# Second norm to up projection: S1 formed from PSUM, S4 in one pass, low parts shared out differently, and the tensor engine's order written out

## The chip, the cores and the metric

The kernel runs on one core of one Trainium2 chip. Five engines of that core work side by side, each through a queue of its own: the tensor engine (PE; its weight loads are listed as PEld), the vector engine (DVE), the scalar engine (ACT), GpSimd (POOL), and SP, which issues the DMAs. The metric is the device time of one execution in microseconds. Before the change it is 2224.81 us, the median of three runs (2224.61 to 2228.78).

## The reference

The program is two layers of an encoder over 1024 tokens of 1024 channels. The part that matters here is the second half of each layer:

```python
x = x + mix @ w_out[l]
h2 = _rmsnorm(x, norm2_g[l])
up = _dwconv3(h2 @ ffn_w_up[l], ffn_conv_w[l])
gate, val = jnp.split(up, 2, axis=-1)
x = x + (jax.nn.silu(gate) * val) @ ffn_w_down[l]
```

`ffn_w_up` has 1024 rows and 2 × 2816 columns. `_dwconv3` is a convolution of three taps along the tokens, one set of taps for each column.

## The kernel before

**Seven products in place of eight.** The product h2 @ W_up is done tile by tile. Tile f (of 22) holds 128 gate columns and the 128 value columns that belong to them. The transposed activations are cut into four quadrants: A11 and A12 are the lower and the upper 512 channels of tokens 0 to 511, A21 and A22 the same channels of tokens 512 to 1023. The weights of a tile are cut likewise: B11 and B21 are the lower and upper channels of the gate columns, B12 and B22 those of the value columns. The scheme is Winograd's form of Strassen's: with S1 = A21 + A22, S2 = S1 − A11, S3 = A11 − A21, S4 = A12 − S2 and T1 = B12 − B11, T2 = B22 − T1, T3 = B22 − B12, T4 = B21 − T2, a tile takes the seven products A11·B11, A12·B21, S1·T1, S2·T2, S3·T3, S4·B22 and A22·T4.

**Three passes for each product.** Each operand is split (`split`, line 114) into a high part, a copy rounded to a narrower type that ACT makes (line 106), and a low part, the rest, a subtraction that DVE or POOL makes (line 117). The kernel multiplies high by high, high by low and low by high (`block_mm`, line 869, its matmuls on line 876): four blocks of 128 channels times three passes, twelve matmuls of 128×512 for each product. They add up in PSUM: S1·T1 and S4·B22 in one bank (`c5`), A11·B11, S2·T2, S3·T3 and A22·T4 in another (`u`), with copies taken in between (`p1`, `u1`, `p5`).

**From the norm to the quadrants.** `norm2_step` (line 822) runs over eight blocks of 128 tokens. For each it does the second half of the output projection (`out_proj`), and, one block behind, the norm (`norm_a`: squares on ACT, line 256, the root on POOL, the multiply on DVE, line 262), and, two blocks behind, `norm2_b` (line 777), which transposes a block through PSUM (line 781) and makes the quadrants. Blocks 0 to 3 give A11 and A12. Blocks 4 to 7 give A22, which is split at once from PSUM, S3 and S2 (DVE, lines 797 and 798), and S1 and S4 (POOL, lines 799 and 800). These sums lie unsplit in two buffers of 8 × 512: `r0` holds A11 and A12, which S1 and S4 overwrite, and `r1` holds S3 and S2. `norm2_end` (line 802) then splits each of S2, S1, S3, S4 in two pieces of 128×1024. Later `r1` serves tile 0 as working storage (`ug`, `uv`, `tg`, `tv`), so that its copies overwrite S2 and S3.

**The weights.** `up_load` (line 836) brings a tile's weights in on SP in two DMAs of 512 KB. `up_prep` (line 852) forms T1 to T4 in place on POOL (line 864; T2 overwrites T1, T4 overwrites B21) and splits them (`up_split`). The low part is made on DVE or on POOL, as the argument `el` says.

**What sets the order.** A planner orders each engine's queue from its own estimates. Within `manual_schedule` the named engines keep the order in which the program is written. `run` (lines 1194 to 1212) does this for DVE, POOL and ACT from block 7's norm to tile 1's weights; the tensor engine's order there is the planner's. In that section tile 0's and tile 1's first two products, which need blocks 0 to 3 alone, are written ahead (`up_ahead`, `up_ahead_copy`), and tile 0 is run as a generator in three parts. What follows, the rest of tile 0 with its convolution (`conv3`, lines 452 to 457) and all other tiles, is ordered by the planner again.

Of the kernel before, what the change touches and what calls it, by code (L numbers as in the profile page):

```python
# [10 lines left out]
AF = mybir.ActivationFunctionType  # L11
ALU = mybir.AluOpType
# [44 lines left out]
class Trunk:  # L57
# [719 lines left out]
    def norm2_b(self, b, xs):  # L777
        nc = self.nc
        pt = self.big()
        for k in range(KC):  # L780
            nc.tensor.transpose(
                pt[:, k * P : (k + 1) * P], xs[:, k * P : (k + 1) * P], self.ident
            )
        pv = pt.rearrange("p (k t) -> p k t", k=KC)
        s = slice((b % 4) * P, (b % 4 + 1) * P)
        r0, r1 = self.raw
        if b == 4:
            self.A["22"] = self.slot(self.xo[0], [2, 4, 512], F32R)
        if b < 4:
            nc.scalar.activation(r0[:, :, s], pv, AF.Copy)  # L790
        for n, k in (("11", 0), ("12", 4)) if b < 4 else (("22", 4),):
            h, l = self.A[n][:, 0, :, s], self.A[n][:, 1, :, s]
            self.split(h, l, pv[:, k : k + 4, :], "a", "v")
        if b >= 4:

            a11, a12, s3, s2 = r0[:, 0:4, s], r0[:, 4:8, s], r1[:, 0:4, s], r1[:, 4:8, s]
            nc.vector.tensor_tensor(out=s3, in0=a11, in1=pv[:, 0:4, :], op=ALU.subtract)
            nc.vector.tensor_tensor(out=s2, in0=pv[:, 4:8, :], in1=s3, op=ALU.subtract)
            nc.gpsimd.tensor_tensor(out=a11, in0=s2, in1=a11, op=ALU.add)
            nc.gpsimd.tensor_tensor(out=a12, in0=a12, in1=s2, op=ALU.subtract)  # L800

    def norm2_end(self, names):

# [18 lines left out]
    def norm2_step(self, b, xs, g, xout):  # L822
        self.out_proj(b, 1)
        self.nc.sync.dma_start(xout[b], self.x[b])
        if b >= 1:
            xs[b - 1] = self.norm_a(b - 1, self.x[b - 1], g, ("G1", "G5"))
        if b >= 2:
            self.norm2_b(b - 2, xs[b - 2])

    def a_op(self, n, k):  # L830
        t = self.A[n]
# [20 lines left out]
    def up_prep(self, f, raws, steps=("11", "T1", "T2", "21", "T3", "22", "T4")):  # L852


        b11, b21, b12, b22 = raws
        B = self.B.setdefault(f, {})
        of = {"11": b11, "T1": b11, "T2": b11, "21": b21, "T3": b12, "22": b22, "T4": b21}
        subs = {"T1": (b12, b11), "T2": (b22, b11), "T3": (b22, b12), "T4": (b21, b11)}
        for n in steps:
            t = n.upper()  # L860
            if t in subs and t not in self.formed.setdefault(f, set()):
                p, q = subs[t]
                self.formed[f].add(t)
                self.nc.gpsimd.tensor_tensor(out=of[t], in0=p, in1=q, op=ALU.subtract)  # L864
            if n == t:
                early = f < 2 and n in ("11", "21")
                B[n] = self.up_split(of[n], "v" if early or n in ("11", "T2", "T3") else "p")

    def block_mm(self, out, a, B, first, last):

# [9 lines left out]

    def up_ahead(self, f, B):

        u, c2 = self.acc("pa"), self.acc(("po", "pf")[f])
        self.block_mm(u, "11", B["11"], True, False)
        self.block_mm(c2, "12", B["21"], True, True)
        return u, c2

    def up_ahead_copy(self, f, u, c2):
        if f == 0:
            self.p1 = self.S(GK)  # L890
        p1 = self.p1[:, f * 512 : f * 512 + 512]
        self.nc.scalar.activation(p1, u, AF.Copy)
        return u, c2, p1

    def up_tile(self, f, B, ahead=None, L=None):

# [2 lines left out]
        nc = self.nc  # L899
# [11 lines left out]
        if ahead:  # L911
            u, c2, p1 = ahead
# [21 lines left out]
        if L is not None:  # L934

            self.order = ExitStack()
            self.order.enter_context(self.tc.manual_schedule(engines={mybir.EngineType.SP}))
            self.down_begin(L)
        self.block_mm(c5, "S4", B["22"], False, True)
        add(uv[:, lo], c5, u1)  # L940
        self.block_mm(u, "22", B["T4"], False, True)
        cp(ug[:, hi], u)

        cg, cv = self.big(), self.big()
        self.conv3(cv, uv, scales(NFF + f))
# [180 lines left out]
    def run(self, depth):  # L1126
# [6 lines left out]
        for L in range(depth):  # L1133
# [57 lines left out]
                elif b == 4:  # L1191
                    self.up_prep(0, raws[0], ("11", "21", "T1", "t2", "t3", "t4"))
            raws[1] += self.up_load(L, 1, (1,))
            with self.tc.manual_schedule(engines=MANUAL):
                xs[7] = self.norm_a(7, self.x[7], g2, ("G1", "G5"))
                ahead.append(self.up_ahead(0, self.B[0]))
                self.up_prep(1, raws[1], ("11", "21"))
                self.norm2_b(6, xs[6])
                ahead[0] = self.up_ahead_copy(0, *ahead[0])
                self.up_prep(0, raws[0], ("T2",))  # L1200
                self.norm2_b(7, xs[7])
                self.up_prep(0, raws[0], ("T3",))
                ahead.append(self.up_ahead(1, self.B[1]))
                ahead[1] = self.up_ahead_copy(1, *ahead[1])
                self.norm2_end(("S2", "S1", "S3"))
                first = self.up_tile(0, self.B[0], ahead[0])
                next(first)
                self.up_prep(0, raws[0], ("22", "T4"))
                self.norm2_end(("S4",))
                self.up_prep(1, raws[1], ("t1",))  # L1210
                next(first)
# [86 lines left out]
```

## Time and profile before

| | |
|---|---|
| median of three runs | 2224.81 us (2224.61 to 2228.78) |
| profiled execution, its own time | 2225.25 us |
| profiled execution, span | 2223.4 us |
| granted tensor clock, mean | 0.999 |
| PE busy | 2202.3 us (99%) |
| DVE busy | 1511.4 us (68%) |
| POOL busy | 1156.9 us (52%) |
| ACT busy | 1106.9 us (50%) |

Times in the profile count from the start of the span. The edited section of layer 0 lies at about 470 to 515 us, that of layer 1 at about 1573 to 1618 us. A row of the timeline gives the start, the length, the engine, the line, the operation, what it writes and reads by the names of the buffers, how many instructions are merged in the row, and in brackets how long its engine was idle before it and what ended that. The names are those of the slots: in this section E and G are weights or pieces of them, H are the large activation buffers, `big`, `pa`, `po` and `pf` are PSUM, and the pieces of S2 lie in W and Z, those of S1 in H, those of S3 and S4 in G and W.

### The profile page before, as it was taken

Reading aid. Unit: us, or ns where it says so; the run is one execution under the profiler, and the core shown is the slowest. Engines: PE = TensorE matmul, PEld = TensorE weight load, DVE = VectorE, ACT = ScalarE, POOL = GpSimd, SP = SyncE. Lnnn points to the kernel's source line nnn. Section 1 sums busy time; section 2 is a strip of 40 time slices with the busy share of each in tenths; the row PEclk is TensorE's granted clock in tenths of the full one; section 3 lists DMA queues with packets and bytes.
Section 4 is the critical chain, followed back from the end, with each engine's and each line's share of the span. In section 5 each row is a group of like instructions: output and inputs, shape, how many; then the busy total and the mean of one; then the engine's idle time right before and its main releaser. Section 6 shows DMA issues by size and latency. Waiting matters only on the chain.

```text
span 2223.4 us, 29441 instructions
## 1 busy us (share of the span) xinstructions
PE 2202.3 (99%) x10590; PEld 1829.1 (82%) x10590; DVE 1511.4 (68%) x1945; ACT 1106.9 (50%) x1879; POOL 1156.9 (52%) x1060
## 2 busy tenths in 40 slices
PE   9999999999999999999999999999999999999999
PEld 7888888877888888888888888888788888888887
DVE  5668887177677777754735688862877777778554
ACT  5247776365444444433432477753545454544332
POOL 5564445577767776020443653556777777751100
PEclk9999999999999999999999999999999999999999
DMA  4100003213545453886520000041235545548754
GB/s 159 45 20 5 16 15 97 109 67 109 167 160 162 156 170 121 296 313 214 203 90 10 20 15 6 21 149 58 76 119 157 171 148 166 161 142 322 281 193 164
DMA packets 202020, 281.91 MB, mean 127 GB/s; under 512 B 15598, under 2 KB 121618, under 8 KB 201874
## 3 DMA queue, kind: packets, MB, share of 16 engines
q1 hardware_dynamic: 201874, 280.03, 37.5%
q8 instruction: 83, 1.36, 0.3%
q14 instruction: 63, 0.52, 0.1%
HBM read 199.77 MB, written 80.22 MB: 126 GB/s over the span
## 4 chain that ended last, share of the span: by engine, by line
PE 85%; POOL 4%; DVE 3%; DMA 3%; issue 2%; ACT 1%; SPq 0%; POOLq 0%; DVEq 0%; ACTq 0%
PE pa L876 17%; PE pf L876 8%; PE big L1075 8%; PE pa L1075 5%; PE pa L638 5%; PE pf L301 5%; PE po L876 4%; PE big L622 3%; PE big L621 3%; PE po L650 3%; PE po L651 3%; PE po L1075 2%; PE pf L1075 2%; PE pa L132 2%; PE pa L130 2%; PE pa L131 2%
## 5 line engine op out<-in xcount | busy, mean ns | idle before, releaser
L630 POOL TENSOR_SCALAR H<-H,rv 128x1024 f32<-128x1024 f32 x128 | 144.6, 1130 | 221.8 <-DVE rv L629 221.8
L876 PE MATMUL pa<-H,E 128*128 128x512 f32 x864 | 212.7, 390 | 1.1 <-DVE H L909 1.1
L643 DVE TENSOR_TENSOR E<-pa,E 128x512 fp32r<-128x512 f32 x256 | 173.4, 688 | 52.2 <-ACT E L642 50.8
L106 ACT ACTIVATE E<-E 128x512 fp32r<-128x512 f32 (+1 forms) x207 | 128.6, 628 | 157.0 <-POOL E L864 72.5
L117 POOL TENSOR_TENSOR E<-E,E 128x512 fp32r<-128x512 f32 (+1 forms) x120 | 176.5, 1475 | 53.0 <-ACT E L106 52.6
L642 ACT ACTIVATE E<-pa 128x512 fp32r<-128x512 f32 x256 | 152.8, 597 | 79.8 <-PE pa L638 78.3
L876 PEld LDWEIGHTS pa<-H,E 128*128 128x128 f32 x864 | 161.6, 188 | 35.3 <-DVE H L909 2.0
L106 ACT ACTIVATE G<-H 128x1024 fp32r<-128x1024 f32 (+1 forms) x116 | 114.1, 1008 | 143.7 <-PE big L1075 73.0
L117 DVE TENSOR_TENSOR G<-H,G 128x1024 fp32r<-128x1024 f32 (+1 forms) x86 | 105.0, 1224 | 110.3 <-ACT G L106 109.9
L624 DVE TENSOR_REDUCE nm<-big 128x1 f32<-128x1024 f32 x128 | 155.7, 1216 | 8.1 <-PE big L622 8.0
L910 ACT ACTIVATE H<-pa 128x512 f32<-128x512 f32 x128 | 75.9, 593 | 167.9 <-PE pa L876 126.7
L638 PEld LDWEIGHTS pa<-ident,H 128*128 128x128 f32 x1024 | 127.1, 140 | 35.4 <-DVE E L643 1.6
L638 PE MATMUL pa<-ident,H 128*128 128x128 f32 x1024 | 154.0, 272 | 0.2
L627 ACT ACTIVATE H<-big,nm 128x1024 f32<-128x1024 f32 x128 | 142.4, 1112 | 12.3 <-DVE nm L624 12.2
L453 DVE SCALAR_TENSOR_TENSOR big<-H,cst,big 128x1023 f32<-128x1023 f32 x44 | 56.6, 1287 | 105.7 <-ACT big L452 105.7
L117 DVE TENSOR_TENSOR E<-E,E 128x512 fp32r<-128x512 f32 (+1 forms) x92 | 96.3, 1055 | 38.2 <-ACT E L106 38.2
L301 PE MATMUL pf<-H,G 128*128 128x512 f32 x288 | 120.1, 431 | 0.0
L876 PE MATMUL pa<-W,E 128*128 128x512 f32 x336 | 116.1, 394 | 0.8 <-ACT H L910 0.5
L994 POOL TENSOR_TENSOR E<-E 128x512 f32<-128x512 f32 x26 | 37.0, 1425 | 140.2 <-DMA E<-in_ffn_w_down_dram 139.9
L106 ACT ACTIVATE G<-E 128x512 fp32r<-128x512 f32 (+2 forms) x110 | 58.5, 546 | 98.2 <-POOL E L864 29.9
L876 PE MATMUL po<-H,E 128*128 128x512 f32 x408 | 104.4, 390 | 0.4 <-ACT E L106 0.4
L864 POOL TENSOR_TENSOR E<-E 128x512 f32<-128x512 f32 x66 | 100.5, 1524 | 3.1
(408 smaller groups left out, 6367.1 us busy)
## 6 DMA issues: line engine op xcount, KB each, us to landing
H<-gdram SPq DMA_DIRECT2D x70, 512.0 KB, 5.6
gdram<-H SPq DMA_DIRECT2D x134, 256.0 KB, 2.5
E<-in_ffn_w_up_dram SPq DMA_DIRECT2D x66, 512.0 KB, 4.4
H<-tdram SPq DMA_DIRECT2D x40, 512.0 KB, 5.2
E<-in_w_in_dram SPq DMA_DIRECT2D x30, 512.0 KB, 3.9
H<-in_ffn_w_down_dram SPq DMA_DIRECT2D x30, 512.0 KB, 4.6
out_dram<-H SPq DMA_DIRECT2D x28, 512.0 KB, 2.9
E<-in_ffn_w_down_dram SPq DMA_DIRECT2D x26, 512.0 KB, 6.4
```

Source lines behind the costliest of these rows:

```text
L106: nc.scalar.activation(out, in_, AF.Copy)
L117: e.tensor_tensor(out=l, in0=src, in1=h.bitcast(F32), op=ALU.subtract)
L301: mm(acc, a[:, k, :], b, start=k + j == 0, stop=k == KC - 1 and j == 2)
L624: nc.vector.tensor_reduce(out=nm, in_=S, op=ALU.max, axis=AX.X, negate=True)
L627: nc.scalar.activation(p, S, AF.Exp, bias=nm, accum_out=sm)
L630: nc.gpsimd.tensor_scalar(out=p, in0=p, scalar1=rv, scalar2=1.0, op0=ALU.mult, op1=ALU.mult)
L638: nc.tensor.transpose(pt[:, r * P : (r + 1) * P], pu[:, r, kc * P : (kc + 1) * P], self.ident)
L642: nc.scalar.activation(hl[:, 0, :], pt, AF.Copy)
L643: nc.vector.tensor_tensor(out=hl[:, 1, :], in0=pt, in1=hl[:, 0, :].bitcast(F32), op=ALU.subtract)
L864: self.nc.gpsimd.tensor_tensor(out=of[t], in0=p, in1=q, op=ALU.subtract)
L876: mm(out, w, x, start=first and k + j == 0, stop=k == 3 and j == 2, skip_group_check=True,)
L1075: nc.tensor.matmul(banks[j], p[:, n, s], r[:, n, :], start=first and n + q == 0 and m < 3, stop=last and n == w - 1 and q == 2, skip_group ...
```

## The change

There are five edits, all in the section between the second norm and the second tile of the up projection, once per layer.

- `norm2_b` for blocks 4 to 7 no longer has POOL add S2 to A11 to get S1. ACT copies A21 out of PSUM over A11, and DVE adds A22 from PSUM to it. S3 and S2 come first, the copy and the addition second, and the split of A22 third. The function is a generator now, so that the three steps can be placed apart.
- S4 is no longer formed block by block. `norm2_s4` subtracts S2 from A12 on POOL in four operations of 128×512, one for each block of channels, after all blocks are done. S4 is split last.
- The low parts of the weights are shared out differently. Tile 0: B11 and B21 on DVE, all others on POOL (T2 and T3 were on DVE). Tile 1: T1, T2, T3 and B22 on DVE, B11, B21 and T4 on POOL (B11, B21, T2 and T3 were on DVE).
- `manual_schedule` covers the tensor engine as well, and `up_ahead` is a generator. The written order is: block 6's transposes, tile 0's two products ahead, block 7's transposes, tile 1's two products ahead, S2·T2, S1·T1.
- In tile 0, A22·T4 comes ahead of S4·B22.

```diff
@@ norm2_b
-        for n, k in (("11", 0), ("12", 4)) if b < 4 else (("22", 4),):
+        for n, k in (("11", 0), ("12", 4)) if b < 4 else ():
             h, l = self.A[n][:, 0, :, s], self.A[n][:, 1, :, s]
             self.split(h, l, pv[:, k : k + 4, :], "a", "v")
         if b >= 4:
-            a11, a12, s3, s2 = r0[:, 0:4, s], r0[:, 4:8, s], r1[:, 0:4, s], r1[:, 4:8, s]
+            a11, s3, s2 = r0[:, 0:4, s], r1[:, 0:4, s], r1[:, 4:8, s]
             nc.vector.tensor_tensor(out=s3, in0=a11, in1=pv[:, 0:4, :], op=ALU.subtract)
             nc.vector.tensor_tensor(out=s2, in0=pv[:, 4:8, :], in1=s3, op=ALU.subtract)
-            nc.gpsimd.tensor_tensor(out=a11, in0=s2, in1=a11, op=ALU.add)
-            nc.gpsimd.tensor_tensor(out=a12, in0=a12, in1=s2, op=ALU.subtract)
+            yield
+            nc.scalar.activation(a11, pv[:, 0:4, :], AF.Copy)
+            nc.vector.tensor_tensor(out=a11, in0=pv[:, 4:8, :], in1=a11, op=ALU.add)
+            yield
+            self.split(
+                self.A["22"][:, 0, :, s], self.A["22"][:, 1, :, s], pv[:, 4:8, :], "a", "v"
+            )
+
+    def norm2_s4(self):
+        r0, r1 = self.raw
+        for k in (6, 5, 4, 7):
+            self.nc.gpsimd.tensor_tensor(
+                out=r0[:, k], in0=r0[:, k], in1=r1[:, k], op=ALU.subtract
+            )
@@ up_prep
-                early = f < 2 and n in ("11", "21")
-                B[n] = self.up_split(of[n], "v" if early or n in ("11", "T2", "T3") else "p")
+                dve = (("11", "21"), ("T1", "T2", "T3", "22"))[f] if f < 2 else ("11", "T2", "T3")
+                B[n] = self.up_split(of[n], "v" if n in dve else "p")
@@ up_ahead (up_ahead_copy is gone)
-        u, c2 = self.acc("pa"), self.acc(("po", "pf")[f])
+        u = self.acc("pa")
         self.block_mm(u, "11", B["11"], True, False)
-        self.block_mm(c2, "12", B["21"], True, True)
-        return u, c2
...
+        yield
         self.nc.scalar.activation(p1, u, AF.Copy)
-        return u, c2, p1
+        yield
+        c2 = self.acc(("po", "pf")[f])
+        self.block_mm(c2, "12", B["21"], True, True)
+        yield u, c2, p1
@@ up_tile
+        if f == 0:
+            self.block_mm(u, "22", B["T4"], False, True)
+            cp(ug[:, hi], u)
         self.block_mm(c5, "S4", B["22"], False, True)
         add(uv[:, lo], c5, u1)
-        self.block_mm(u, "22", B["T4"], False, True)
-        cp(ug[:, hi], u)
+        if f > 0:
+            self.block_mm(u, "22", B["T4"], False, True)
+            cp(ug[:, hi], u)
@@ run
-            with self.tc.manual_schedule(engines=MANUAL):
+            with self.tc.manual_schedule(engines=MANUAL | {mybir.EngineType.PE}):
                 xs[7] = self.norm_a(7, self.x[7], g2, ("G1", "G5"))
-                ahead.append(self.up_ahead(0, self.B[0]))
                 self.up_prep(1, raws[1], ("11", "21"))
-                self.norm2_b(6, xs[6])
-                ahead[0] = self.up_ahead_copy(0, *ahead[0])
+                part = [self.norm2_b(b, xs[b]) for b in (6, 7)]
+                next(part[0])
+                next(part[0])
+                begun = [self.up_ahead(f, self.B[f]) for f in range(2)]
+                next(begun[0])
+                next(begun[0])
+                ahead.append(next(begun[0]))
                 self.up_prep(0, raws[0], ("T2",))
-                self.norm2_b(7, xs[7])
+                next(part[1])
+                next(part[0], None)
+                next(part[1])
+                self.norm2_end(("S2",))
                 self.up_prep(0, raws[0], ("T3",))
-                ahead.append(self.up_ahead(1, self.B[1]))
-                ahead[1] = self.up_ahead_copy(1, *ahead[1])
-                self.norm2_end(("S2", "S1", "S3"))
+                next(begun[1])
+                next(begun[1])
+                ahead.append(next(begun[1]))
+                self.norm2_s4()
+                self.up_prep(0, raws[0], ("T4", "22"))
+                self.norm2_end(("S1",))
+                next(part[1], None)
+                self.norm2_end(("S3",))
                 first = self.up_tile(0, self.B[0], ahead[0])
                 next(first)
-                self.up_prep(0, raws[0], ("22", "T4"))
                 self.norm2_end(("S4",))
                 self.up_prep(1, raws[1], ("t1",))
                 next(first)
```

4 lines of the change are left out of this document (2 added, 2 removed).

## The prediction

> **What bounds the kernel now.** I read the page first.
>
> ```profile
> span 2223.4 us, 29441 instructions
> PE 2202.3 (99%) x10590; PEld 1829.1 (82%) x10590; DVE 1511.4 (68%) x1945; ACT 1106.9 (50%) x1879; POOL 1156.9 (52%) x1060
> ```
>
> The tensor engine is busy 99% of the span, so an edit to other engines is worth only what it takes out of the tensor engine's waits. Next I took the busy time by windows around the edited code: the stretch from the first matmul of tile 0's "11" product to the first matmul of tile 1's S2·T2, in layer 0 and in layer 1, and then slices of it.
>
> ```profile
> 478.88:513.00 34.12, 30.71 (x139) 23.61 (x137) 32.60 (x31) 21.14 (x32) 25.05 (x17) 1.00 0.21 62
> 1582.30:1616.05 33.75, 31.51 (x139) 25.02 (x138) 30.84 (x31) 19.78 (x29) 23.72 (x16) 0.95 0.20 63
> ...
> 474.00:478.00 4.00, 4.00 (x19) 3.30 (x18) 3.75 (x4) 0.93 (x2) 2.90 (x4) 1.00 0.32 131
> ...
> 490.00:494.00 4.00, 2.38 (x10) 1.41 (x8) 3.88 (x4) 3.17 (x4) 4.00 (x4) 1.00 0.00 0
> ...
> 502.00:506.00 4.00, 3.34 (x12) 2.10 (x12) 4.00 (x3) 0.57 (x1) 3.40 (x2) 1.00 0.81 228
> ...
> 1598.00:1602.00 4.00, 4.00 (x12) 3.13 (x11) 4.00 (x4) 2.41 (x3) 0.70 (x1) 0.57 0.00 0
> ```
>
> The columns are time, then busy time of PE, PEld, DVE, ACT, POOL, granted clock, DMA. Here DVE is the full engine (32.60 of 34.12 us), and PE has holes (2.38 of 4.00). The timeline of layer 0 (start, length, engine) shows what the holes wait for:
>
> ```profile
> 478.88 2.58 PEld L876 LDWEIGHTS pa<-H,E 128*128 128x128 f32 x12
> ...
> 481.77 1.29 DVE L262 SCALAR_TENSOR_TENSOR G<-H,rsx,E 128x1024 f32<-128x1024 f32 x1
> ...
> 482.98 3.48 DVE L117 TENSOR_TENSOR E<-E,E 128x512 fp32r<-128x512 f32 x2
> ...
> 485.56 0.60 ACT L106 ACTIVATE H<-big 128x512 fp32r<-128x512 f32 x1 [3.69 <-PE big L781]
> ...
> 486.06 1.02 PEld L781 LDWEIGHTS big<-ident,G 128*128 128x128 f32 x8
> ...
> 487.05 2.14 PEld L876 LDWEIGHTS pa<-H,E 128*128 128x128 f32 x10
> ...
> 488.29 0.68 DVE L117 TENSOR_TENSOR E<-E,E 128x512 fp32r<-128x512 f32 x1
> ...
> 490.08 1.30 POOL L800 TENSOR_TENSOR H<-H,H 128x512 f32<-128x512 f32 x1
> ...
> 490.20 0.69 DVE L798 TENSOR_TENSOR H<-big,H 128x512 f32<-128x512 f32 x1
> ...
> 490.93 2.01 ACT L106 ACTIVATE W<-H 128x1024 fp32r<-128x1024 f32 x2 [0.68 <-DVE H L798]
> ...
> 492.02 4.37 DVE L117 TENSOR_TENSOR Z<-H,W 128x1024 fp32r<-128x1024 f32 x2
> ...
> 493.02 2.28 POOL L800 TENSOR_TENSOR H<-H,H 128x512 f32<-128x512 f32 x1
> ...
> 494.20 0.50 PE L876 MATMUL pa<-Z,E 128*128 128x512 f32 x1 [1.66 <-DVE Z L117]
> ...
> 496.31 2.35 DVE L117 TENSOR_TENSOR H<-H,H 128x1024 fp32r<-128x1024 f32 x2
> ...
> 504.18 2.30 DVE L117 TENSOR_TENSOR G<-H,G 128x1024 fp32r<-128x1024 f32 x1
> ...
> 504.31 0.50 PE L876 MATMUL big<-G,G 128*128 128x512 f32 x1 [0.55 <-DVE G L117]
> ...
> 508.01 2.68 PEld L876 LDWEIGHTS pa<-H,E 128*128 128x128 f32 x12
> ...
> 510.74 2.23 PEld L876 LDWEIGHTS po<-H,E 128*128 128x128 f32 x10
> ...
> 513.00 0.19 PEld L876 LDWEIGHTS pa<-W,E 128*128 128x128 f32 x1
> ```
>
> Each hole ends with a DVE low part (L117): Z is S2's, G is S3's or S4's. The ceiling: twelve matmuls take 508.01 to 510.74, 0.2275 us each; eight transposes 486.06 to 487.05, 0.99 us. The stretch holds ten products of twelve matmuls (27.3 us) and sixteen transposes (2.0 us), 29.3 us of work. Lost are 34.12 − 29.3 = 4.8 us in layer 0 and 33.75 − 29.3 = 4.45 us in layer 1, together 9.3 us, 0.42% of the span.
>
> The rows also price contention. Two subtractions of 1024 elements, both inputs in SBUF, take 4.37 us while POOL subtracts (492.02) and 2.35 us when POOL is idle (496.31). POOL's own subtraction takes 1.30 us (490.08) or 2.28 us (493.02). A DVE subtraction with one input in PSUM takes 0.69 us even during POOL's (490.20). So the first two kinds take turns: one POOL and one DVE operation together need about 2.28 us. I call that a pair.
>
> **The change, part by part.** All times are worked out on layer 0's clock; layer 1 runs the same code.
>
> *S1 out of PSUM.* Per layer four POOL additions (L799, 1.3 to 2.3 us) go; four ACT copies (0.60, the row at 485.56) and four DVE additions with a PSUM input come, costed as L798, 0.69. For blocks 4 and 5 they fall before 478.88, where PE is fully busy with the output projection (row 474): nothing; uncovered they would cost 1.3 us a block. For blocks 6 and 7 they are in the chain below. The copy adds a wait: ACT must let DVE read the old value first. Behind it on ACT stand tile 0's p1 copy and T2's high part, which nobody needs before 491.
>
> *Tensor order.* Block 6's transposes now come first: 478.88 to 479.9. Tile 0's "11" and "12" products: 24 × 0.2275 = 5.46, to 485.3. Block 7's transposes to 486.3. Tile 1's two products to 491.8. From there S2·T2 is next.
>
> *DVE until S2.* Tile 1's two low parts (3.48 us at 482.98) and tile 0's T2, T3 low parts (0.68 at 488.29, if free) leave DVE for POOL. The norm's multiply (481.77) ends by about 483.4, behind a POOL low part. s3, s2 of block 6 and, after ACT's copy, the addition: 485.5. Then DVE idles until block 7's transposes end at 486.3: s3, s2, block 6's "22" low part, addition, at 0.6 each: 488.7. S2's low parts, 2 × 1.17, uncontended: 491.0, against 496.4 now. The 1.66 us hole is gone: S2·T2 runs 491.8 to 494.5.
>
> *The queue behind it.* ACT: S2's high parts 487.6 to 489.6 (2.01 for two), T3's, p1, T4's, "22"'s at 0.60 to 492.0, S1's first high part at 493.0. POOL: S4's four subtractions could start at 487.6, but stand behind T3's low part, which waits for ACT until 490.2 and for DVE's turn until 491.0: done 492.3. Then S4 at 493.6, and, now in pairs, 495.9, 498.2, 500.4; T4's low part 502.7, "22"'s 504.9, forming tile 1's T1 507.2. DVE in the same pairs: S1's low parts 494.6 and 496.8; S3's 499.1 and 501.4; S4's 503.6 and 505.9. ACT's u1 copy overwrites what S4's first subtraction reads; that ends at 493.6, the copy is due at 496.6: no wait.
>
> *PE then.* S1·T1 stops halfway for its second low part: 0.9. S3·T3 waits 0.9 at its start and 0.9 halfway, and ends at 502.7. A22·T4, now ahead of S4, ends at 505.4; S4·B22 at 508.1, its operands in time by 0.4 to 0.9. Tile 1's T1 high and low parts (0.6, 0.68) end at 508.6, a wait of 0.2; S1·T1 of tile 1 ends at 511.0. Now: 513.00. The waits are 2.9 instead of 4.8 us.
>
> *What is late next.* T2 of tile 1 is formed over T1's buffer, so after T1's low part.
>
> ```profile
> 500.97 2.62 SPq L842 DMA_DIRECT2D E<-in_ffn_w_up_dram  x2
> ...
> 505.43 0.63 ACT L106 ACTIVATE E<-E 128x512 fp32r<-128x512 f32 x1 [3.46 <-POOL E L864]
> ...
> 507.47 0.63 ACT L106 ACTIVATE E<-E 128x512 fp32r<-128x512 f32 x1 [1.40 <-DMA E<-in_ffn_w_up_dram]
> ...
> 507.71 1.29 POOL L864 TENSOR_TENSOR E<-W,E 128x512 f32<-128x512 f32 x1
> ...
> 508.91 1.12 ACT L452 ACTIVATE big<-H,csth 128x1024 f32<-128x1024 f32 x1 [0.81 <-DVE H L909]
> ...
> 510.06 1.29 DVE L453 SCALAR_TENSOR_TENSOR big<-H,csth,big 128x1023 f32<-128x1023 f32 x1 [0.52 <-ACT big L452]
> ...
> 511.26 1.24 DVE L117 TENSOR_TENSOR E<-E,E 128x512 fp32r<-128x512 f32 x1
> ...
> 511.79 0.58 ACT L910 ACTIVATE H<-pa 128x512 f32<-128x512 f32 x1
> ```
>
> After: 508.6 + 1.29 (POOL) + 0.63 (ACT) + 0.68 (DVE) = 511.2, against 512.5 now (511.26 + 1.24); PE wants it at 511.0 + 0.45. If one convolution step of tile 0 gets ahead on ACT (1.12) and DVE (1.29) and POOL holds a turn, it is 513.0: a wait of 1.6. So the wait lies between 0 and 1.6. Against it: tile 2's "11" product can fill in, as its bank is freed by the u copy of A22·T4, now 511.79, then about 506. Its weights (issued on SP at 500.97, landed 507.47) follow tile 0's last low parts: T4's at 502.7 is as early as now, "22"'s at 504.9 is 4 us later, but only tile 2's T1 needs that half. I take 0.6, nearer to the filled end. Tile 1's S2·T2 then starts at 511.6: 1.4 us gained in layer 0 (2.0 to 0.4). Layer 1's stretch is 0.37 us shorter now and I give it the same end: 1.0 us (1.6 to 0). Sum 2.4 us, with ends 3.6 and 0.4.
>
> Layer 1's half clock (0.57 in the last slice) is no term of its own: that layer lost less in all, because PE ran slowly where it would have waited. The Trainium skill (TensorE: Matmul & The Clock Gate, "What's actually happening") states that the half rate returns after a whole idle window of about 3.4 us. This trace differs: it came in layer 1 although a matmul was issued amid the waits. By the page no wait above would call it; by the trace one could, which is a rival below.
>
> The profiled execution took 2225.25 us, 0.44 above the runs' median of 2224.81. 2225.25 − 2.4 − 0.44 = **2222.4 us**; with the ends, 2221.2 to 2224.4.
>
> **Rivals.**
> 1. *Most of the ceiling is won.* If the turns fall better (POOL's S4 done while ACT makes S1's high parts, when DVE idles from 491.0 to 493.0 anyway), each pair that falls apart takes a 0.9 us wait with it, and the fill hides T2. At 1.5 us lost per layer: 9.3 − 3.0 = 6.3 gained, 2218.5. For it: POOL is idle for 2.6 us just before. Against: the pairs from 492 to 507 are back to back.
> 2. *T2 of tile 1 takes it all.* One convolution step ahead and no fill: 0.4 us gained, 2224.4.
> 3. *Slower.* Tile 1's T2 low part lands behind all four convolution steps of tile 0 on DVE, since that order is the scheduler's. From 510.4, 4 × 1.29 and one more ACT step end near 515.6, the low part at 516.3, and S2·T2 effectively starts at 515.9: 2.9 and 3.3 us later than now, 2231.0; with tile 2's product (2.7 us) as fill 2225.6. It decides from the second step ahead of T2 on. For it: DVE has two low parts more there (T1, "22"). Against: they stand earlier in the program.
> 4. *The clock halves in both layers* on the 0.9 us waits: as in the slice at 0.57, 0.43 × 4 = 1.7 us each at most: 2225.8. Against: layer 0 kept 1.00 through a 1.66 us wait.
>
> **From cases to numbers.** Forecast 0.33, rivals 0.27, 0.18, 0.12, 0.10. Less than 0.2% (4.45 us) can't be told from no change. Faster, under 2220.4: rival 1 and the forecast's best part, 0.35. Slower, over 2229.3: rival 3 mostly, 0.12. Same: 0.53. The range 2217.0 to 2228.0 leaves out a tenth on each side: the last of rival 1 and the unfilled end of rival 3.
>
> **What would show it.** Right: in layer 0 S2's low parts (Z) end near 491 at 1.2 us each, no wait at S2·T2, four S4 subtractions on POOL of which three take about 2.28 us, waits near 0.9 at S1·T1 and S3·T3, tile 1's S2·T2 starting at 511 to 512. Wrong: low parts of S1 and S3 at 1.2 us each (rival 1), a wait of over 1.6 us before tile 1's S2·T2 (rivals 2, 3), a granted clock under 1.00 near 500 (rival 4), or a gain or loss outside this stretch, in which case the scheduler moved something that I left alone.

## The result, and the profile after

The changed kernel is slower: 2237.64 us (median of five executions, 2235.0 to 2240.79) against 2225.99 us for the kernel before on the same chip, a ratio of 1.0057 with an interval of 1.0046 to 1.0068. The forecast was 2222.4 us, with a range of 2217.0 to 2228.0. The profiled execution is the longest of the five: 2240.79 us, a span of 2238.9 us against 2223.4. The page of the changed kernel:

```profile
span 2238.9 us, 29455 instructions
...
PE 2206.6 (99%) x10590; PEld 1830.8 (82%) x10590; DVE 1508.8 (67%) x1949; ACT 1111.2 (50%) x1887; POOL 1156.2 (52%) x1056
```

No engine has noticeably more work. The span grew by 15.5 us and PE's busy time by 4.3, so PE waits more, and part of what it does runs slower. To find where, I cut each layer into two stretches by counting weight loads. **Stretch A** runs from the end of the output projection to the first matmul of tile 1's S2·T2 (the end of the prediction's stretch). **Stretch B** is the next 156 matmuls, thirteen products; it ends inside tile 3. The windows for the kernel before (A and B of layer 0, then of layer 1; columns: window, time, busy PE, PEld, DVE, ACT, POOL, granted clock, DMA):

```profile
477.89:513.00 35.11, 31.70 (x146) 24.51 (x144) 33.45 (x32) 21.14 (x32) 26.04 (x17) 1.00 0.20 60
513.00:548.49 35.49, 35.49 (x157) 29.20 (x156) 28.95 (x28) 18.19 (x28) 26.26 (x20) 1.00 0.40 126
1581.31:1616.04 34.73, 32.49 (x145) 25.91 (x144) 31.67 (x32) 19.77 (x29) 24.70 (x16) 0.95 0.20 61
1616.04:1652.17 36.13, 35.66 (x157) 29.21 (x156) 29.52 (x28) 19.34 (x31) 27.32 (x21) 1.00 0.39 124
```

and for the changed kernel, with one early window at the end:

```profile
479.50:517.11 37.61, 32.34 (x146) 24.49 (x145) 32.12 (x31) 22.98 (x36) 26.78 (x17) 1.00 0.18 56
517.11:557.12 40.01, 37.29 (x158) 30.34 (x157) 29.16 (x30) 18.29 (x28) 26.27 (x19) 0.96 0.35 112
1590.02:1627.61 37.59, 32.34 (x146) 24.49 (x145) 32.12 (x31) 22.95 (x36) 26.78 (x17) 1.00 0.18 57
1627.61:1667.59 39.98, 37.26 (x158) 30.35 (x157) 29.15 (x30) 18.28 (x28) 26.27 (x19) 0.96 0.34 112
8.00:30.00 22.00, 18.81 (x84) 14.57 (x83) 14.86 (x16) 11.49 (x20) 9.54 (x12) 0.92 0.70 261
```

Stretch A lost 2.5 and 2.9 us, stretch B 4.5 and 3.85: 13.7 us. Another 1.6 us is lost near 20 us, where the granted clock of this execution was 0.92 for 22 us (479.50 − 477.89). The tensor engine's queue there is the same in both kernels, so this is not the change's doing. That makes 15.3 of the 15.5 us. So **more than half of the loss lies in stretch B, after the edited section**, where the prediction had put nothing. The waits of PE (what was waited for, us in total, times, longest), changed kernel:

```profile
PE pa L890 <- ACT H L924: 5.4, 2, 2.7
...
PE big L781 <- DVE H L117: 2.8, 4, 1.2
```

The product matmuls stand on line 890 now (876 before). The first row is stretch B's, one wait a layer; the second is block 7's transposes with others of its kind. The kernel before had 0.5 us of the first kind, and 3.7 us of waits for S2's low parts, which are gone:

```profile
PE pa L876 <- DVE Z L117: 3.7, 3, 1.7
...
PE pa L876 <- ACT H L910: 0.5, 1, 0.5
```

**Stretch B.** The timeline of the changed kernel around its long wait:

```profile
536.14 2.88 PE L890 MATMUL pa<-H,E 128*128 128x512 f32 x12
...
539.06 0.60 ACT L924 ACTIVATE H<-pa 128x512 f32<-128x512 f32 x1 [4.44 <-PE pa L890]
...
548.22 1.22 DVE L975 TENSOR_TENSOR H<-big,H 128x1024 f32<-128x1024 f32 x1
...
549.48 0.60 ACT L924 ACTIVATE H<-pa 128x512 f32<-128x512 f32 x1 [1.40 <-DVE H L975]
...
550.13 0.19 PEld L890 LDWEIGHTS pa<-W,E 128*128 128x128 f32 x1 [3.14 <-ACT H L924]
550.13 0.50 PE L890 MATMUL pa<-W,E 128*128 128x512 f32 x1 [2.72 <-ACT H L924]
```

and the same place before:

```profile
529.54 2.88 PE L876 MATMUL pa<-H,E 128*128 128x512 f32 x12
...
532.46 0.60 ACT L910 ACTIVATE H<-pa 128x512 f32<-128x512 f32 x1 [0.64 <-PE pa L876]
...
542.49 0.60 ACT L910 ACTIVATE H<-pa 128x512 f32<-128x512 f32 x1 [3.04 <-DVE H L956]
...
543.14 0.19 PEld L876 LDWEIGHTS pa<-W,E 128*128 128x128 f32 x1 [0.26 <-ACT H L910]
```

The first row of each is A22·T4 of tile 1, that tile's last product. Behind it runs a chain: the copy of `u`, the convolution, the gate, and the product of gate and value (L975, before L956). Only then may the `p1` copy of tile 3 overwrite the buffer, and tile 3's S2·T2 waits for that copy. From the `u` copy to S2·T2 it is 10.7 us before (532.46 to 543.14) and 11.1 after (539.06 to 550.13). The chain is as long as it was; what PE has to do meanwhile has shrunk. The tensor queue of the two built kernels, from tile 2's S2·T2 on (tile in brackets):

```
before  S2·T2(2)  A22·T4(1)  A12·B21(2)  S4·B22(2)  A11·B11(3)  A12·B21(3)  S2·T2(3)
after   S2·T2(2)  A12·B21(2) x11  A22·T4(1)  A12·B21(2) x1  S4·B22(2)  A11·B11(3)  A12·B21(3)  S2·T2(3)
```

Before, four products (10.9 us) stand between the two ends of the chain; after, three and one matmul (8.4 us). The wait of 3.14 us is followed by the half clock (0.50 from 552 to 554 us, row further below). For B of layer 0 that gives 3.14 − 0.26 = 2.9 us of waiting and 40.0 × (1 − 0.96) = 1.6 us of clock, together the measured 4.5.

**Stretch A.** The timeline of the changed kernel, only the rows that decide:

```profile
487.85 0.69 DVE L117 TENSOR_TENSOR H<-big,H 128x512 fp32r<-128x512 f32 x1
...
488.68 1.06 PE L781 MATMUL big<-ident,G 128*128 128x128 f32 x8 [1.19 <-DVE H L117]
...
491.81 2.00 ACT L106 ACTIVATE W<-H 128x1024 fp32r<-128x1024 f32 x2
...
492.89 2.36 DVE L117 TENSOR_TENSOR Z<-H,W 128x1024 fp32r<-128x1024 f32 x2 [0.26 <-ACT W L106]
...
494.84 0.19 PEld L890 LDWEIGHTS pa<-W,E 128*128 128x128 f32 x1
...
496.37 8.00 POOL L811 TENSOR_TENSOR H<-H,H 128x512 f32<-128x512 f32 x4
...
496.83 4.16 DVE L117 TENSOR_TENSOR H<-H,H 128x1024 fp32r<-128x1024 f32 x2 [1.58 <-ACT H L106]
...
503.15 2.31 DVE L117 TENSOR_TENSOR W<-H,G 128x1024 fp32r<-128x1024 f32 x1
...
507.74 0.19 PEld L890 LDWEIGHTS big<-G,E 128*128 128x128 f32 x1 [1.01 <-DVE G L117]
...
508.87 0.30 PEld L890 LDWEIGHTS big<-W,E 128*128 128x128 f32 x2 [0.94 <-POOL E L117]
...
511.75 0.30 PEld L890 LDWEIGHTS po<-H,E 128*128 128x128 f32 x2 [0.75 <-ACT E L106]
```

S2's low parts (Z) take 1.18 us each and S2·T2 starts at 494.84 without a wait: the old hole is closed. But block 7's transposes wait 1.2 us for the last reader of block 5's PSUM tile (487.85), S4's pass on POOL takes 8.00 us beside S1's and S3's low parts, which take over 2 us each, and PE stops at S4·B22 twice, the second time for B22's low part (L117 on POOL, behind S4's pass), and at tile 1's T1.

### The profile page after: what moved, and what is told of

Same layout as the page of the kernel before. It is cut to its first block, busy times and chain, and to the rows that moved or that the text cites. A ratio compares the mean times of both kernels' runs of the same rounds, so it can differ in the third digit from the quotient of the medians.

```text
span 2238.9 us, 29455 instructions
## 1 busy us (share of the span) xinstructions
PE 2206.6 (99%) x10590; PEld 1830.8 (82%) x10590; DVE 1508.8 (67%) x1949; ACT 1111.2 (50%) x1887; POOL 1156.2 (52%) x1056
## 4 chain that ended last, share of the span: by engine, by line
PE 81%; issue 5%; POOL 5%; DMA 3%; DVE 3%; ACT 1%; SPq 0%; POOLq 0%; ACTq 0%; DVEq 0%
PE pa L890 18%; PE pf L890 8%; PE pa L638 5%; PE pf L301 5%; PE po L890 4%; PE big L1094 4%; PE pa L1094 4%; PE big L622 3%; PE big L621 3%; PE po L650 3%; PE po L651 3%; PE pa L130 2%; PE pa L132 2%; PE pa L131 2%; PE pf L1094 2%
## 5 line engine op out<-in xcount | busy, mean ns | idle before, releaser
L117 POOL TENSOR_TENSOR E<-E,E 128x512 fp32r<-128x512 f32 (+1 forms) x124 | 183.3, 1483 | 66.1 <-ACT E L106 65.8
L890 PE MATMUL pa<-H,E 128*128 128x512 f32 x840 | 206.4, 390 | 2.1 <-DVE H L923 2.1
L117 DVE TENSOR_TENSOR G<-H,G 128x1024 fp32r<-128x1024 f32 (+1 forms) x86 | 105.1, 1226 | 108.8 <-ACT G L106 108.4
L117 DVE TENSOR_TENSOR E<-E,E 128x512 fp32r<-128x512 f32 (+1 forms) x88 | 88.9, 1017 | 43.7 <-ACT E L106 43.4
```

The lines of the kernel that those rows point to most:

```text
L117: e.tensor_tensor(out=l, in0=src, in1=h.bitcast(F32), op=ALU.subtract)
L890: mm(out, w, x, start=first and k + j == 0, stop=k == 3 and j == 2, skip_group_check=True,)
```

## The experiments

The table holds, for each kernel, stretch A and B of both layers in its profiled execution (from the starts of its weight loads), its median, and the ratio to the kernel before on the same chip. Between them the kernels before had medians of 2225.29 to 2225.99. All stretches are cut at the same count of weight loads. In a_s4 and c_new two matmuls of tile 2 stand ahead of tile 1's S2·T2, and in a_t0 its first matmul stands one place earlier, so there the cut lies up to two matmuls beside the start of that product.

| kernel | A, layers 0 / 1 | B, layers 0 / 1 | median us | ratio (interval) |
|---|---|---|---|---|
| before | 35.11 / 34.73 | 35.49 / 36.13 | 2225.99 | 1 |
| after | 37.61 / 37.59 | 40.01 / 39.98 | 2237.64 | 1.0057 (1.0046–1.0068) |
| a_dep | 37.57 / 37.56 | 35.47 / 35.45 | 2231.17 | 1.0021 (1.0012–1.0031) |
| a_sh | 37.49 / 38.68 | 36.28 / 36.23 | 2231.88 | 1.0027 (1.0016–1.0038) |
| b_sh | 36.53 / 36.57 | 41.21 / 38.39 | 2236.33 | 1.0052 (1.0038–1.0066) |
| a_s4 | 35.30 / 35.31 | 36.49 / 36.47 | 2227.06 | 1.0007 (0.9997–1.0016) |
| a_s1 | 36.15 / 36.23 | 40.02 / 38.36 | 2234.16 | 1.0040 (1.0025–1.0055) |
| b_s1 | 37.84 / 37.63 | 35.49 / 35.49 | 2230.67 | 1.0025 (1.0015–1.0035) |
| a_b5 | 39.50 / 39.53 | 38.36 / 39.98 | 2242.83 | 1.0078 (1.0063–1.0093) |
| a_pe | 39.93 / 40.23 | 38.40 / 35.36 | 2240.32 | 1.0070 (1.0055–1.0085) |
| b_pe | 35.11 / 34.70 | 35.49 / 36.17 | 2225.46 | 1.0001 (0.9992–1.0010) |
| a_t0 | 42.73 / 42.22 | 35.46 / 35.45 | 2241.96 | 1.0074 (1.0061–1.0086) |
| c_new | 36.33 / 36.51 | 35.48 / 35.49 | 2227.26 | 1.0009 (1.0001–1.0018) |
| c_old | 37.05 / 37.83 | 36.28 / 36.27 | 2231.72 | 1.0027 (1.0018–1.0036) |

**Is the place of one product the cause of stretch B?** In a_dep two products of tile 2 may be issued only after tile 1's A22·T4. Nothing else differs from the changed kernel.

```diff
-            self.block_mm(c2, "12", B["21"], True, True)
+            with self.tc.issue_after(self.mm22.ins) if f == 2 else ExitStack():
+                self.block_mm(c2, "12", B["21"], True, True)
...
-        self.block_mm(c5, "S4", B["22"], False, True)
+        with self.tc.issue_after(self.mm22.ins) if f == 2 else ExitStack():
+            self.block_mm(c5, "S4", B["22"], False, True)
...
-            self.block_mm(u, "22", B["T4"], False, True)
+            self.mm22 = self.block_mm(u, "22", B["T4"], False, True)
```

> The changed kernel with one edge of order added: tile 2's products A12·B21 and S4·B22 may be issued only after tile 1's A22·T4. On the tensor engine's queue this moves tile 1's A22·T4 ahead by one product, and nothing else up to tile 3; every engine has the same work. Theory 'order': the 3.1 us wait before tile 3's S2·T2 comes from that one place in the queue, because tile 1's last product starts the chain u copy, convolution, gate, and tile 3's p1 copy overwrites what that chain reads. The wait falls under 0.6 us in both layers, and the half-clock stretch behind it goes too: 7 to 8.5 us less than the changed kernel, 2229 to 2231. Rival 'backlog': DVE is late with tile 1's convolution because it got two more low parts of tile 1, wherever the product stands: the wait stays over 2.5 us, 2236 to 2239.

The timeline of a_dep at the same place:

```profile
533.78 2.88 PE L890 MATMUL pa<-H,E 128*128 128x512 f32 x12
...
536.70 0.60 ACT L925 ACTIVATE H<-pa 128x512 f32<-128x512 f32 x1 [1.95 <-PE pa L890]
```

and its window for layer 0's stretch B:

```profile
517.24:552.71 35.47, 35.47 (x158) 29.21 (x157) 28.65 (x30) 18.27 (x28) 26.50 (x19) 1.00 0.39 126
```

A22·T4 starts without a wait behind tile 2's S2·T2, so its operands had been there: the order had held it back, not its data. Stretch B is back at 35.5 us in both layers, PE busy throughout, at full clock. The profiled span fell by 8.8 us (2238.9 to 2230.1), the median by 6.5, a little less than the 7 to 8.5 expected; the executions of the changed kernel differ in mean clock (0.997 to 1.000), and their median lies below the profiled one.

**Which edit moved that product?** a_sh takes the new sharing of low parts back out of the changed kernel; b_sh puts it alone into the kernel before.

```diff
-                dve = (("11", "21"), ("T1", "T2", "T3", "22"))[f] if f < 2 else ("11", "T2", "T3")
-                B[n] = self.up_split(of[n], "v" if n in dve else "p")
+                early = f < 2 and n in ("11", "21")
+                B[n] = self.up_split(of[n], "v" if early or n in ("11", "T2", "T3") else "p")
```

> The changed kernel with the old sharing of low parts (tiles 0 and 1: B11, B21, T2, T3 on DVE, T1, B22, T4 on POOL). The queue of the tensor engine then has tile 1's A22·T4 ahead of most of tile 2's A12·B21. Theory 'order': the wait before tile 3's S2·T2 is gone, 7 to 8.5 us less than the changed kernel, about 2229 to 2231; the loss up to tile 1's S2·T2 (2.3 us a layer) stays. Rival 'pairs': the loss up to tile 1's S2·T2 comes from POOL's low parts taking turns with DVE, so giving them back to DVE also cuts that loss by 1 us or more a layer: 2225 to 2228.

> The kernel before with the new sharing of low parts alone. Its tensor queue shows tile 1's A22·T4 behind eleven of tile 2's A12·B21, as in the changed kernel. Theory 'order': a wait of about 3 us before tile 3's S2·T2 in each layer, 6 to 8.5 us more than before, 2231 to 2235. Rival: the sharing costs nothing by itself and the loss needs the new S1 and S4: 2224 to 2228, no such wait.

a_sh has B at 36.3 us, b_sh at 41.2 and 38.4. In the built b_sh the queue reads as in the changed kernel, eleven matmuls of A12·B21(2) ahead of A22·T4(1); in a_sh three of them stand there. So the sharing, through the planner, makes most of the loss of the whole change by itself: b_sh alone is 0.52% slower, and 8.0 us of that lie in B. (PE stands 2.7 us before tile 3's S2·T2 in both layers of b_sh; B differs between them because the granted clock over B was 0.92 in layer 0 and 1.00 in layer 1.) Its A rose too, by 1.4 and 1.8 us, and the cause of that was not tried. In a_sh A did not fall (37.5, and 38.7 in layer 1), so the rival that POOL's low parts make A long did not hold. Why the planner's estimates come out so was not tried.

**What does S4's single pass cost?** a_s4 is the changed kernel with S4 formed block by block again, right after S2.

```diff
             nc.vector.tensor_tensor(out=s2, in0=pv[:, 4:8, :], in1=s3, op=ALU.subtract)
+            a12 = r0[:, 4:8, s]
+            nc.gpsimd.tensor_tensor(out=a12, in0=a12, in1=s2, op=ALU.subtract)
             yield
...
-                self.norm2_s4()
```

> The changed kernel with S4 formed block by block again (POOL subtracts right behind each block's S2), and no S4 pass at the end. Stretch A is the time from the last output projection matmul to tile 1's S2·T2 on the tensor engine: 35.1 and 34.7 us before, 37.6 and 37.6 changed. Theory 'cover': before, POOL's subtractions ran while DVE worked from PSUM, which does not take turns with POOL; the one pass puts four of them beside DVE's low parts of S1 and S3, where each costs a turn. Undone, those low parts take about 1.2 us again instead of 2.3, and stretch A falls by 2 to 3 us a layer, to 34.6 to 35.6. Rival 'bank': the loss comes from block 7's transposes, which wait 1.5 us for block 5's bank; stretch A stays within 0.7 us of 37.6.

The timeline of a_s4, S3's second low part:

```profile
502.38 1.21 DVE L117 TENSOR_TENSOR W<-H,G 128x1024 fp32r<-128x1024 f32 x1
```

It takes 1.21 us, as do both of S4's, where the changed kernel has 2.3. A falls by 2.3 us, to within 0.6 us of the kernel before. Formed by block, S4 of blocks 6 and 7 ran beside DVE work that reads PSUM (1.28 and 1.30 us on POOL); in one pass it takes turns with low parts that PE waits for. B is 36.5 too: the one edit moves the planner's order as well.

**What does S1 out of PSUM cost?** a_s1 gives S1 back to POOL in the changed kernel, b_s1 takes it out of PSUM in the kernel before.

```diff
-            nc.scalar.activation(a11, pv[:, 0:4, :], AF.Copy)
-            nc.vector.tensor_tensor(out=a11, in0=pv[:, 4:8, :], in1=a11, op=ALU.add)
+            nc.gpsimd.tensor_tensor(out=a11, in0=s2, in1=a11, op=ALU.add)
```

> The changed kernel with S1 formed on POOL again from S2 and A11, all else as changed. DVE loses four additions a layer, POOL gets four. Theory 'cover': two more POOL operations near DVE's low parts cost up to two turns of about 1 us; block 5's and 6's banks are given back about 1 us earlier. Together stretch A between 37 and 39 us. Rival: the new S1 is itself what costs (ACT's copy and DVE's addition hold the banks): stretch A under 36.5.

> The kernel before with S1 formed out of PSUM alone (ACT copies A21, DVE adds A22, in place of POOL's addition). Theory 'bank': the readers of a block's bank run one after the other, so the copy and the addition lengthen the time for which the bank is held by about 1.4 us a block; blocks 6 and 7 and S2 come later, stretch A rises by 1 to 2 us a layer, 2227 to 2230. Rival 'cover': POOL loses two operations that took turns with DVE's low parts, and stretch A falls by 0.5 to 2 us, 2221 to 2224.5.

A falls by 1.4 us in a_s1, as the rival had it, and rises by 2.7 and 2.9 in b_s1, more than the 1 to 2 expected. The timeline of a_s1 has block 7's transposes without a wait:

```profile
485.87 1.05 PE L781 MATMUL big<-ident,G 128*128 128x128 f32 x8
```

That of b_s1 has its loss at S2·T2, for S2's high part, which ACT makes late:

```profile
494.07 0.80 PE L877 MATMUL pa<-W,E 128*128 128x512 f32 x1 [3.74 <-ACT W L106]
```

Part of the rise in b_s1 is the clock that went with this wait: the granted clock over A was 0.91 in both layers. So S1 out of PSUM costs time in both surroundings, at another place in each.

**Is it block 5's PSUM tile?** a_b5 writes block 5's quadrants at the head of the ordered section, ahead of block 7's norm, so that the tile comes free early.

```diff
-            for _ in self.norm2_b(b - 2, xs[b - 2]):
-                pass
+            if b < 7:
+                for _ in self.norm2_b(b - 2, xs[b - 2]):
+                    pass
...
+                for _ in self.norm2_b(5, xs[5]):
+                    pass
                 xs[7] = self.norm_a(7, self.x[7], g2, ("G1", "G5"))
```

> The changed kernel with block 5's quadrants (S3, S2, S1, split of A22) written into the ordered section, ahead of block 7's norm. Block 5's bank is then given back before block 7's transposes want it. Theory 'bank': the 1.5 us wait before block 7's transposes goes, what follows comes earlier by as much, stretch A falls by 1.0 to 1.5 us a layer, to 36.1 to 36.6. Rival 'cover': the wait goes, but the turns of POOL and DVE set the end anyway, and stretch A stays within 0.5 us of 37.6.

It got worse, A by 1.9 us in both layers. The timeline of a_b5, block 5's readers in their order, then the norm and block 7's transposes:

```profile
479.88 0.68 DVE L797 TENSOR_TENSOR H<-H,big 128x512 f32<-128x512 f32 x1
...
480.59 0.69 DVE L798 TENSOR_TENSOR H<-big,H 128x512 f32<-128x512 f32 x1
...
481.37 0.60 ACT L800 ACTIVATE H<-big 128x512 f32<-128x512 f32 x1 [2.74 <-DVE H L798]
...
482.00 0.69 DVE L801 TENSOR_TENSOR H<-big,H 128x512 f32<-128x512 f32 x1 [0.72 <-ACT H L800]
...
482.73 0.60 ACT L106 ACTIVATE H<-big 128x512 fp32r<-128x512 f32 x1 [0.76 <-DVE H L801]
...
483.36 0.69 DVE L117 TENSOR_TENSOR H<-big,H 128x512 fp32r<-128x512 f32 x1 [0.66 <-ACT H L106]
...
485.31 2.30 DVE L262 SCALAR_TENSOR_TENSOR G<-H,rsx,E 128x1024 f32<-128x1024 f32 x1 [1.26 <-POOL rsx L125]
...
487.66 1.09 PE L781 MATMUL big<-ident,G 128*128 128x128 f32 x8 [1.60 <-DVE G L262]
```

The tile is free at 484.05 and no longer waited for; now the transposes wait for the norm, whose square on ACT starts at 483.22, behind block 5's high part. The rows show the cost that I had left out: six reads in strict turn, DVE, DVE, ACT, DVE, ACT, DVE, each engine idle while the other reads, 4.2 us without any other work. In the kernel before the split came first and there were four reads, 2.6 us in its timeline (479.19 to 481.83), of which these are the first and the last:

```profile
479.19 0.60 ACT L106 ACTIVATE H<-big 128x512 fp32r<-128x512 f32 x1 [4.26 <-PE big L781]
...
481.14 0.69 DVE L798 TENSOR_TENSOR H<-big,H 128x512 f32<-128x512 f32 x1
```

The Trainium skill (PSUM — Partial Sum Buffer, "PSUM bank collisions raise a hardware error") states that two engines must not read one bank at once and that software has to keep them apart; the high part's wait for the addition (0.76 us idle) agrees with that. The copy reads the other half of the tile and waited all the same; why was not tried.

**What is the written tensor order worth?** a_pe leaves the tensor engine to the planner again in the changed kernel, b_pe writes its order in the kernel before; the edit is the one word in `run`.

```diff
-            with self.tc.manual_schedule(engines=MANUAL | {mybir.EngineType.PE}):
+            with self.tc.manual_schedule(engines=MANUAL):
```

> The changed kernel with the tensor engine's order in the section left to the planner again. Theory 'cover': the order of the tensor engine is not what costs in stretch A: within 0.7 us of 37.6. Rival 'order written': in order, the transposes of block 7 stand behind 24 matmuls and DVE waits for them; planned, stretch A falls by over 1 us. The wait at tile 3 stays in both, since the planner's queue still has tile 1's A22·T4 behind eleven matmuls of tile 2's A12·B21.

> The kernel before with the tensor engine's order written out alone: the section's program order (tile 0's two products, block 6's and block 7's transposes, tile 1's two products, S2·T2, S1·T1) binds the tensor engine; nothing else is changed. Leaving that order to the planner cost the changed kernel 2.3 to 2.6 us of stretch A a layer. If the written order is worth the same here, stretch A falls from 35.1 and 34.7 to 32.5 to 33.5 us and the time to 2221 to 2223. Rival: before, S2 was late on DVE itself (its low parts end at 496.4), so the order of the tensor engine changes little: stretch A within 0.7 us, 2224.5 to 2227.

In a_pe A rises by 2.3 and 2.6 us, which neither the theory nor the rival had; in b_pe it stays, as the rival had it. The timeline of a_pe:

```profile
491.25 1.03 PE L781 MATMUL big<-ident,G 128*128 128x128 f32 x8
...
495.45 0.50 PE L890 MATMUL pa<-W,E 128*128 128x512 f32 x1 [1.78 <-ACT W L106]
```

Left to the planner, block 7's transposes come late, behind eighteen of the twenty-four matmuls of tile 1's two products, where the written order has them ahead of all twenty-four. S2's chain starts late, and S2·T2 waits. In the kernel before, those transposes were early enough already. So this edit pays for part of what the others cost.

**Would a written order for the rest of tile 0 help?** The prediction had A22·T4 fill the time in which S4's low parts are made. In the built queue it does not: S4·B22 still comes first, then two matmuls of tile 1, then A22·T4. a_t0 keeps the tensor engine's written order to the end of tile 0.

```diff
+                written = ExitStack()
+                if f < WRITTEN:
+                    written.enter_context(
+                        self.tc.manual_schedule(engines={mybir.EngineType.PE})
+                    )
                 for _ in tile_steps:
                     pass
+                written.close()
```

> The changed kernel with the tensor engine's order written for the rest of tile 0 too, so that A22·T4 really stands ahead of S4·B22 (in the changed kernel's queue it still stands behind S4·B22 and two matmuls of tile 1). The planner then also puts tile 1's A22·T4 ahead of tile 2's A12·B21. Theory 'order': A22·T4 covers the waits for S4's second low part and B22's low part, 1.5 to 2 us a layer, and the wait at tile 3 is gone, 3.9 to 4.5 a layer: 2225 to 2228. Rival 'backlog': only the first part is won, 2233 to 2236.

A rose by 5.1 and 4.6 us, so this failed. The timeline of a_t0:

```profile
511.34 1.15 ACT L107 ACTIVATE E<-E 128x512 fp32r<-128x512 f32 x2 [5.09 <-POOL E L879]
...
512.02 0.50 PEld L891 LDWEIGHTS po<-H,E 128*128 128x128 f32 x2 [5.21 <-ACT E L107]
512.02 1.22 PE L891 MATMUL po<-H,E 128*128 128x512 f32 x2 [4.78 <-DVE H L924]
```

Two matmuls of tile 1's S1·T1 had slipped in ahead of A22·T4, where nothing of tile 1 was written. They need tile 1's T1, whose high part ACT makes from what POOL forms behind S4's pass and two low parts, and PE stood still for 4.78 us. So the swap itself has not been tried with A22·T4 truly first, and its worth stays open. Stretch B was 35.5 us here.

**Do the good parts add up?** c_new keeps the written order and the new sharing with a_dep's edge, and forms S1 and S4 by block on POOL. c_old does the same with the old sharing and no edge. Their diffs are those of a_dep, a_s1 and a_s4, and of a_sh, a_s1 and a_s4.

> What the runs so far leave of the change: written order of the tensor engine, new sharing of low parts, tile 1's A22·T4 held ahead of tile 2's A12·B21 and S4·B22; S1 and S4 formed block by block on POOL as before. If the parts add up, stretch A is 37.6 − 2.3 (S4) − 1.4 (S1) = 33.9 us, against 35.1 and 34.7 before, and the stretch from there to tile 3 is 35.5, as before: 2 to 3 us less than before, 2222 to 2224. Rival: the two savings overlap, since both come out of the same queue on DVE and POOL: stretch A 34.8 to 35.5, no change.

> The same with the old sharing of low parts and no edge of order: the kernel before with only the written order of the section's engines changed. Stretch A 33.5 to 35 us if the sharing is worth little there; over 35.5 if POOL needs the help that the new sharing gives. The stretch from there to tile 3 should be 35.5 to 36.3, since the planner's queue has most of tile 2's A12·B21 behind tile 1's A22·T4. 2222 to 2227.

c_new's A is 36.3 and 36.5 us, worse than a_s4's 35.3, although S1 on POOL by itself had gained 1.4 in a_s1. Neither the 33.9 expected nor the rival's 34.8 to 35.5 came. The windows of c_new's A:

```profile
477.81:514.14 36.33, 32.88 (x146) 25.53 (x144) 29.45 (x29) 20.68 (x31) 29.47 (x20) 0.95 0.19 58
1581.73:1618.24 36.51, 33.66 (x145) 26.88 (x144) 29.62 (x29) 20.84 (x32) 29.65 (x21) 0.91 0.19 59
```

Here S1·T1 waits 1.96 us for S1's high part on ACT, and the half clock goes with that wait: 36.33 × 0.05 = 1.8 and 36.51 × 0.09 = 3.3 us of clock, where a_s4 had 1.00 in both layers. At full clock some of that would have been waiting instead, so whether the waits saved add up is not known. In time, the parts do not. c_old's A of 37.1 and 37.8 us is in line with its forecast for the case that POOL needs the help of the new sharing (over 35.5), but with clocks of 0.95 this is not shown either, and it took 2231.72 us against 2222 to 2227 expected. No kernel here beats the kernel before; a_s4, b_pe and c_new lie within 0.1% of it.

## Why the prediction was wrong

**The ceiling** held: PE's waits were the matter, and no engine's busy time changed what came out.

**"Tensor order" and "DVE until S2"** were right in kind. S2's low parts ran uncontended at 1.18 us (1.17 forecast) and the hole of 1.66 us went. But S2·T2 began 15.3 us after the stretch's start (479.50), not 13.9 (477.89 to 491.8). The step that failed is *"Block 7's transposes to 486.3"*, reached without a wait, and under it *"for blocks 4 and 5 they fall before 478.88, where PE is fully busy: nothing"*. In the changed kernel everything up to the section came 1.6 us later, so I take that off its times in this section. Block 5's readers ended at 486.9 (488.54), long after 478.88, and block 7's transposes, which need that tile, waited 1.2 us; block 6's had already waited 0.2 us for block 4's. The profile before could have told it: block 5's four readers ran from 479.19 to 481.83 there, behind the point at which I had them done. I had counted instructions for engines and never asked when the PSUM tile comes free. Undoing S1 removes this wait and 1.4 us of A.

**"The queue behind it"**: the pairs came as worked out. S4's four subtractions took 8.00 us, S1's low parts 4.16 for two, S3's second 2.31. The Trainium skill (SBUF — State Buffer, "Who interferes with whom") has a DVE instruction with two SBUF inputs and a GpSimd instruction that reads SBUF exclude each other; the trace agrees, with 2.3 us shared and 1.21 alone. But the start was wrong. S2's high parts began at 490.2 on ACT (491.81 in the trace), not 487.6, T3's stood behind them, T3's low part on POOL behind that, and S4's pass began at 494.8 (496.37), not 492.3.

**"PE then"**: the wait halfway in S1·T1 and the two in S3·T3 were there, about 1.0 us each against 0.9, and one more at S1·T1's first low part. *"A22·T4, now ahead of S4, ends at 505.4; S4·B22 at 508.1, its operands in time"* failed outright: the planner left S4·B22 in front, and two waits of about 1 us came there. Tile 1's T1 cost 0.75 us against 0.2. From the start of S2·T2 to the end of A it took 22.3 us (494.84 to 517.11) where the prediction had 19.8 (491.8 to 511.6). I took the order in the source for the order in the queue, for a product outside the section in which the order is written.

**"What is late next"** named T2 of tile 1. It was not late: S2·T2 of tile 1 began at 517.10 without a wait, and tile 2's A11·B11 filled in behind its first two matmuls, as argued. Rivals 2 and 3 therefore did not happen, and rival 1 did not either; that rival 3 also said slower is chance, as its mechanism played no part. Rival 4's clock drop did not come on the 1 us waits in A.

In stretch A this makes a loss of 2.5 and 2.9 us where I had a gain of 1.4 and 1.0: 7.8 of the 17.9 us between the profiled execution (2240.79) and the forecast on the same footing (2225.25 − 2.4). The early clock is 1.6. Nearly all of the rest, 8.4, is **stretch B**, which no step of the sum and no rival held. It stood only as the last item under "What would show it": a loss outside the stretch, "in which case the scheduler moved something that I left alone". I named it and gave it no chance and no price. Yet the kernel's text said that all tiles after the section are ordered by the planner, and the profile before had the warning in it: tile 3's S2·T2 already stood 0.26 us for its copy, at the end of a chain of 10.7 us covered by 10.9 us of products. One product's shift was enough to break that cover.

## What to carry to other kernels

Where a planner orders part of a queue, an edit that only moves work to another engine can reorder products it never touches: compare the built queues, and look in the trace before for chains that are covered with almost nothing to spare. For an operation that is moved onto a PSUM operand, ask first when the tile comes free and who waits for it, since readers on two engines may go strictly in turn. Judge each part of a compound edit by its own stretch of the tensor engine, as the parts can cancel and need not add, and read the granted clock of each stretch with it.

## What was not expected of the hardware

**The half clock came after shorter waits than I had thought, and not after every one of them.** The window of the changed kernel after its 2.72 us wait in layer 0 (the one from 1662 us, after the same wait in layer 1, has 0.50 too):

```profile
552.00:554.00 2.00, 2.00 (x6) 1.52 (x5) 1.45 (x3) 0.03 (x1) 0.00 (x0) 0.50 0.88 333
```

In a_pe, waits of 1.78 and 0.76 us with one matmul between them were followed by it too (498 to 500 us: 0.50). The Trainium skill (TensorE: Matmul & The Clock Gate, "What's actually happening") puts the half rate behind an idle window of about 3.4 us; these waits are shorter, so this case differs. The same wait can go either way. PE stood 2.7 us before tile 3's S2·T2 in both layers of the changed kernel, b_sh, a_s1 and a_b5 and in layer 0 of a_pe. Five of these nine waits had the half clock with them, and four had not (layer 1 of b_sh and a_s1, layer 0 of a_b5 and a_pe). That is why B is 40 to 41 us in the five and 38.4 us in the four. So a wait of about 2 us or more has to be counted with a possible loss, some 1.6 us here. The waits of about 1 us in stretch A of the changed kernel were not followed by it, with 1.00 over both stretches.

**The same opening does not always keep its clock.** Between 18 and 22 us the granted clock was 0.64 in the profiled execution of the changed kernel, 0.62 in a_dep's, 0.61 in a_pe's and 0.63 in a_t0's, but full in the kernel before and the nine others, with the same tensor queue up to there. All fourteen have a wait of 1.2 to 1.9 us at about 18 us, the longest of them (c_new, 1.90 us) with the full clock behind it. The half clock there costs 1.6 us, and what decides it stays open.
